# Four edits to a fp32 hybrid S5 / short-conv layer: the head's order, where six small loads are issued, how two tables lie in DRAM, and which engines do the last norms

## The chip, the cores and the metric

One NeuronCore of a Trainium2 chip runs the whole kernel. TensorE (PE) multiplies, VectorE (DVE), ScalarE (ACT) and GpSimd (POOL) work on vectors, and SyncE (SP), ACT and POOL issue DMAs. The metric is the device time of one execution in microseconds (us), as the median of several runs; less is better.

## The reference, cut to what matters

One layer of a latent generator: 512 latent rows `x` and 256 context rows `ctx` of 2048 channels, all fp32.

```
shift, scale, gate = split(silu(c) @ w_ada + b_ada)        # and the same for c_ctx
h  = layernorm(x)   * (1 + scale)   + shift                # (512, 2048)
hc = layernorm(ctx) * (1 + scale_c) + shift_c              # (256, 2048)
u, z_s5, v, bg, cg, z_cv = split(h @ w_in);  u_c = hc @ w_in[:, :1024]
# S5, 64 groups of 16 channels, 64 complex states, two directions
a_bar = exp(lam * dt);  b_bar = (a_bar - 1) / lam * b
states = scan(a_bar, b_bar, u), begun from the last context state
y_s5 = glu(Re(C states) + D u);  y_cv = bg * dwconv3(cg * v)
o = concat(y_s5 * silu(z_s5), y_cv * silu(z_cv)) @ w_out
out = layernorm(2**0.25 * x + gate * o) * ln_g + ln_b      # (512, 2048)
```

## The kernel before, in words

Every fp32 product is made of three matmuls on a high and a low part of either operand (`hi`/`lo` of the activations, `whi`/`wlo` of the weights). A weight tile arrives in `raw`, ScalarE copies it to `whi`, VectorE subtracts to get `wlo`. The weights of all projections form one list, `items`; SP loads them into five `raw` buffers in that order. Behind the head a planner with a cost model (`_Clock`) decides at build time where the vector work goes between the matmuls, so on the chip every engine runs a fixed list. All instructions pass through one helper line, so the profile gives nearly every one the same line, L137; tiles tell them apart.

**The head** (`head()`) is ordered by hand. Six row tiles are loaded into a ring of seven 1-MiB buffers (`wa`): four of `x`, two of `ctx`, and between and behind them the 32 pieces of the adaLN weights, two for each of the 16 channel blocks k. `stats(q)` are BN_STATS and the square root of row tile q, `norm(q)` the reciprocal steps and the scaling `wa<-wa`, `turn(q)` 16 PE transposes with their copies to `xl` or `xc`. `ada(k, hf)` multiplies a weight piece by silu(c) into `aps`; `combine(k)` copies that (`part`), transposes it and makes shift and scale (`ss`); `mod(k)` makes the high and low part of block k. `lat(k)` and `cxt(k, hf)` are the u projection of latent and context rows. A buffer of the ring is loaded again when its user has been issued (`fill`). `s5_params` (some hundred small VectorE instructions) is trickled into the loop over k by `some(us)`, ends in a table `PI`, whose transposes `WT` are stored to DRAM as `Wd`.

**Phase W** (`phase_w`) follows the head while PE works through the conv weights. For each of eight channel blocks i and of real and imaginary part r, `load_w` reads `pwt` from `Wd` and `load_b` reads `btt` from an input, 512 KB each and issued by POOL. In both, rows of 4 KB are repeated over partitions: the innermost contiguous run is 1024 floats, and the outer dimensions are [8 rows, 16 repeats] for `pwt` and [8 repeats, 16 rows] for `btt`. VectorE multiplies them into `wr`, `wi` (with `tm`), and PE makes the states. u passes through DRAM as `Ud`: ACT stores `ut`, POOL loads `uu`.

**The end.** `epi(q, b)` forms the residual of row tile q and column block b with its BN_STATS, `final(q)` normalizes the four blocks and stores them.

Of the kernel before, what the change touches and what calls it, by code (L numbers as in the profile page):

```python
# [8 lines left out]
F32 = mybir.dt.float32  # L9
# [3 lines left out]
OP = mybir.AluOpType  # L13
# [12 lines left out]
ALPHA = 2.0 ** 0.25  # L26
EPS = 1e-6
MAGIC = 12582912.0


class _Clock:
# [111 lines left out]
def tile_hybrid_s5_shortconv(  # L143
# [21 lines left out]
        return [dram.tile(shape, F32, name=f"{nm}{i}") for i in range(8)]  # L165

    Ud, Kd = spill("Ud", [L, P, NU]), spill("Kd", [2, P, 15 * H])
    Wd = dram.tile([L, 2, NG, P], F32, name="Wd")
    Gd, Zd, Od = spill("Gd", [P, 8, NCH]), spill("Zd", [P, SEQ]), spill("Od", [P, SEQ])

    hc_cm = pool(name="hc", bufs=1, side="right")
# [19 lines left out]
    def tt(out, a, b, op, e=None):  # L191
        (e or ve).tensor_tensor(out, a, b, op=op)
# [112 lines left out]
    def s5_params(hp, cps, lam, room):  # L305
# [146 lines left out]
        for j in range(4):  # L452
# [2 lines left out]
                pe.transpose(cps[:, n * P:(n + 1) * P], PI[:, 2 * j + n].rearrange("p r g -> p (r g)"), ident)  # L455
            ac.activation(WT[:, 2 * j:2 * j + 2], cps.rearrange("p (s c) -> p s c", s=2), AF.Copy)
            yield 0
        ac.dma_start(Wd.rearrange("s r g c -> (r g) s c"), WT)


    def head():
        with pool(name="head", bufs=1) as hp, \
                pool(name="hps", bufs=1, space=bass.MemoryType.PSUM) as ps:
            c2 = ss[:, :, 0]
            sp.dma_start(c2, c2_in)
            jp = ones.bitcast(I32)
            gp.iota(jp, pattern=[[1, P]], base=0, channel_multiplier=-1)
# [29 lines left out]
                load()  # L497
            lam = hp.tile([P, 3, NG], F32, name="lam")
            for t, src in ((bss, b_ss), (lam, lam_in), (cvw, cv_w), (cvb, cv_b), (bgl, b_glu), (dsk, dsk_in)):
                ac.dma_start(t, src)  # L500
            acc = [ps.tile([P, 512], F32, name=f"acc{i}") for i in range(7)]
            aps = ps.tile([P, 512], F32, name="aps")
            aps, cps = aps[:, 0:256], aps[:, 256:512]
# [7 lines left out]
            def stats(q):  # L511
                stt = hp.tile([P, 4, 6], F32, name="bst", tag="bst", bufs=2)
                mv = hp.tile([P, 2], F32, name="mv", tag="mv", bufs=3)
                for f in range(4):
                    ve.bn_stats(stt[:, f], rows["x", q][:, f * 512:(f + 1) * 512])
                    yield
                ve.bn_aggr(mv, stt)
                sts[q] = mv
                rss[q] = rstd_a(hp, mv[:, 1:2], epst)
                yield  # L520

            def norm(q):
                yield from rstd_b(rss[q], sts[q][:, 1:2])
                t = rows["x", q]
                ve.tensor_scalar(t, t, sts[q][:, 0:1], rss[q][:, 3:4], op0=OP.subtract, op1=OP.mult)

            def run(*gs):
                gs = list(gs)
                while gs:
                    for g in list(gs):  # L530
                        try:
                            next(g)
                        except StopIteration:
                            gs.remove(g)

            def turn(q):
                t = rows["x", q]
                for k4 in range(4):
                    b = acc[(4 * q + k4) % 7 if q < 4 else 3 + k4]
                    for k in range(4):  # L540
                        kk = k4 * 4 + k
                        pe.transpose(b[:, k * P:(k + 1) * P], t[:, kk * P:(kk + 1) * P], ident)
                    for k in range(4):
                        kk = k4 * 4 + k
                        dst = xl[kk][:, q * P:(q + 1) * P] if q < 4 else xc[kk][:, (q - 4) * P:(q - 3) * P]
                        if q == 5 and k % 2:
                            ve.tensor_copy(dst, b[:, k * P:(k + 1) * P])
                        else:
                            ac.activation(dst, b[:, k * P:(k + 1) * P], AF.Copy)
                used.add(("x", q))  # L550
                fill()

            def ada(k, hf):
                w = rows[k, hf].rearrange("p (k c) -> p k c", k=8)
                for j in range(8):
                    pe.matmul(aps[32 * (j % 4):32 * (j % 4) + 32], cs[:, hf * 8 + j], w[:, j],
                              start=hf == 0 and j < 4, stop=hf == 1 and j > 3)
                used.add((k, hf))
                fill()
# [43 lines left out]
            def mod_l(k):  # L603
                mod(k, [lpart])

            def mod_c(k):
                mod(k, [cpart])

            def split(n):
                while st["split"] < n:  # L610
                    j = st["split"]
                    hi, lo = pair()
                    r = raws.pop(j)
                    ac.activation(hi, r, AF.Copy)
                    tt(lo, r, hi.bitcast(F32), OP.subtract)
                    his[j] = (hi, lo)
                    st["split"] += 1

            run(stats(0))
            run(norm(0))  # L620
            run(stats(1))
# [3 lines left out]
            run(norm(2), stats(3))  # L625
            turn(2)
            ada(0, 0)
            run(norm(3))
            ada(0, 1)
            turn(3)  # L630
            comb = {k: combine(k) for k in range(KT)}
            next(comb[0])
            split(1)
            next(comb[0])
            mod_l(0)
            run(stats(4))
            ada(1, 0)
            ada(1, 1)
            next(comb[1])
            run(norm(4), stats(5))  # L640
            turn(4)
            lat(0, *his[0])
            next(comb[1])
            mod_l(1)
            split(2)
            run(norm(5))
            ada(2, 0)
            turn(5)
            lat(1, *his[1])
            ada(2, 1)  # L650
            next(comb[2])
            mod_c(0)
            split(3)
            next(comb[2])
            mod_l(2)
            mod_c(1)
            mod_c(2)
            lat(2, *his[2])
            cxt(0, 0, *his.pop(0))
            ada(3, 0)  # L660
            cxt(1, 0, *his.pop(1))
            ada(3, 1)
            next(comb[3])
            cxt(2, 0, *his.pop(2))
            ahead(3)
            next(comb[3])
            mod_l(3)
            mod_c(3)
            st["pos"] = 3
            params = s5_params(hp, cps, lam, lambda: (13, 0) in used)  # L670

            def some(us):
# [15 lines left out]
                cxt(k, hf, *w)  # L688
                st["pos"] += 1

            for k in range(4, KT):
                ada(k, 0)
                ada(k, 1)
                next(comb[k])
                half()
                if k == 4:
                    half()
                next(comb[k])
                half()
                mod(k, [lpart, cpart], lambda: some(1.3))  # L700
                some(1.3)
            while st["pos"] < 2 * KT:
                half()
                some(2.6)
# [35 lines left out]


    OB, uc = {}, {}
    head_order = [(k, hf) for hf in range(2) for k in range(3)] + [(k, hf) for k in range(3, KT) for hf in range(2)]
    for k, hf in head_order:
        add(w_u[k, :, hf * 512:(hf + 1) * 512], None)

# [201 lines left out]
    def phase_w():  # L948
# [5 lines left out]

        def load_w(i, r):
            pt[i, r] = s5.tile([P, 8, P], F32, name="pwt", tag="pwt", bufs=3)
            src = Wd[:, r, 8 * i:8 * i + 8]
            gp.dma_start(pt[i, r], bass.AP(tensor=src.tensor, offset=src.offset, ap=[[2 * NG * P, L], [0, H], [1, 8 * P]]))

        def load_b(i, r):  # L960
            bt[i, r] = s5.tile([P, 8, P], F32, name="btt", tag="btt", bufs=3)
            src = bt_in[i, :, r]
            gp.dma_start(bt[i, r], bass.AP(tensor=src.tensor, offset=src.offset, ap=[[0, L], [16 * P, H], [1, 8 * P]]))

        def states(i, wt):
            u = uu.pop(i)
# [359 lines left out]
    def final(q):  # L1326
        mv = cvp.tile([P, 2], F32, name="omv", tag="omv", bufs=2)
        ve.bn_aggr(mv, bst[:, q])
        sd = rstd_a(cvp, mv[:, 1:2], epst)
        yield 0  # L1330
        for _ in rstd_b(sd, mv[:, 1:2]):
            pass
        rs = sd[:, 3:4]
        nb = cvp.tile([P, 1], F32, name="onb", tag="onb", bufs=2)
        ve.scalar_tensor_tensor(nb, mv[:, 0:1], -1.0, rs, op0=OP.mult, op1=OP.mult)
        yield 0
        for b in (3, 0, 1, 2) if q > 2 else range(4):
            r = R[q, b]
            if q < 3 or b == 3:
                ac.activation(r, r, AF.Identity, scale=rs, bias=nb)  # L1340
                tt(r, r, lg[b], OP.mult, ve if q < 3 else gp)
                tt(r, r, lb[b], OP.add, gp)
            else:
                ve.scalar_tensor_tensor(r, r, mv[:, 0:1], lg[b], op0=OP.subtract, op1=OP.mult)
                ve.scalar_tensor_tensor(r, r, rs, lb[b], op0=OP.mult, op1=OP.add)
            sp.dma_start(out[q * P:(q + 1) * P, b * 512:(b + 1) * 512], r)
            yield 0

# [12 lines left out]
def _layout(inputs):  # L1361
# [32 lines left out]
    def bpar(re, im, perm):  # L1394
# [21 lines left out]
        "b_glu": asc(hg(g["b_glu"][0], 0).reshape(8, P).T),  # L1416
        "lam": asc(lam),
        "b": bpar(g["s5_b_re"], g["s5_b_im"], (1, 3, 0, 2, 4)),
        "bt": asc(np.stack([g["s5_b_re"][0], g["s5_b_im"][0]]).reshape(2, 2, 8, 8, 64, H)
                  .transpose(2, 5, 0, 3, 1, 4).reshape(8, H, 2, 8, P)),  # L1420
        "ct": asc(np.stack([c_ri, c_ri[::-1]]).transpose(1, 5, 2, 0, 3, 4).reshape(P, 2, 2, 8, 8, H)
                  .transpose(0, 3, 1, 2, 4, 5)),
        "dsk": dsk.reshape(P, 8, 2),
# [23 lines left out]
```

## Time and profile before

| | |
|---|---|
| median of 3 runs (1017.64 to 1020.67) | 1018.48 us |
| the profiled execution's own time | 1022.81 us |
| its span in the profile | 1021.0 us |
| mean granted TensorE clock | 0.969 |
| PE busy | 933.2 us (91%) |
| DVE busy | 674.8 us (66%) |
| ACT busy | 378.9 us (37%) |
| POOL busy | 146.6 us (14%) |
| HBM read, written | 177.37 MB, 16.12 MB |

The span is the profiled execution from its first to its last event; 1.8 us of its own time lie outside it. A share of 91% for PE says that the kernel as a whole is bound by TensorE; the other 88 us are a few waits, and where they lie decides what an edit elsewhere can give. The clock is the one granted by the throttle, 1.0 being 2.4 GHz and 0.5 being 1.2 GHz.

### The profile page before, as it was taken

The numbers are of one execution on the slowest core, as the hardware profiler recorded it, in microseconds if no ns is written. First come the engines' busy times: TensorE is split into PE (matmuls) and PEld (weight loads), VectorE is DVE, ScalarE is ACT, GpSimd is POOL, SyncE is SP. The second block draws the span as 40 slices with busy tenths as digits, with TensorE's granted clock in tenths as the row PEclk, the third lists the DMA queues.
The fourth block names the chain that finished last, engine by engine and source line by source line (L and its number), as shares of the span: only waits on it lengthen the run. The fifth ranks groups of instructions, "written<-read, shape, count | busy, mean of one in ns | idle before, by whom it ended". The sixth has DMA issues, their size and how long they took to land.

```text
span 1021.0 us, 15369 instructions
## 1 busy us (share of the span) xinstructions
PE 933.2 (91%) x5488; PEld 755.1 (74%) x5488; DVE 674.8 (66%) x1540; ACT 378.9 (37%) x671; POOL 146.6 (14%) x270
## 2 busy tenths in 40 slices
PE   2569799979999899999999999999999999999990
PEld 2447576857878788888888888888878877778780
DVE  5546995425877779989857556661245789782676
ACT  2523233313444332223345545465434432222321
POOL 0101040111112000000121202111200023300044
PEclk9879999989999999999999999999999999999996
DMA  8958774599899933333473735664686678854412
GB/s 322 364 186 332 284 299 148 147 231 225 201 220 183 214 98 113 105 109 114 126 201 100 212 85 165 153 165 127 181 276 215 226 260 306 309 158 152 145 67 99
DMA packets 104237, 194.53 MB, mean 191 GB/s; under 512 B 33376, under 2 KB 40672, under 8 KB 99296
## 3 DMA queue, kind: packets, MB, share of 16 engines
q1 hardware_dynamic: 69280, 110.14, 36.2%
q0 software_dynamic: 21328, 75.53, 24.8%
q10 hardware_dynamic: 13552, 7.88, 2.6%
q8 instruction: 43, 0.70, 0.3%
q14 instruction: 34, 0.28, 0.1%
HBM read 177.37 MB, written 16.12 MB: 190 GB/s over the span
## 4 chain that ended last, share of the span: by engine, by line
PE 68%; DVE 14%; DMA 10%; issue 4%; ACT 2%; SPq 0%; ACTq 0%; POOL 0%; DVEq 0%; POOLq 0%
PE mm L137 50%; PE bg L137 10%; PE acc L137 6%; DMA Ud<-ut 4%; DMA btt<-in_bt_dram 3%; DVE res L137 3%; PE aps L137 2%; DVE wlo L137 2%; DVE pt L137 2%; DVE tm L137 1%; DMA pwt<-Wd 1%; DVE bst L137 1%; DMA graw<-Gd 1%; DVE lo L137 1%; DMA wa<-in_x_dram 1%
## 5 line engine op out<-in xcount | busy, mean ns | idle before, releaser
L137 ACT ACTIVATE whi<-raw 128x512 fp32r<-128x512 f32 x276 | 171.5, 630 | 335.0 <-PE mm L137 225.6
L137 DVE TENSOR_TENSOR wlo<-raw,whi 128x512 fp32r<-128x512 f32 x276 | 188.2, 692 | 160.4 <-ACT whi L137 151.4
L137 PE MATMUL mm<-hi,wlo 128*128 128x512 f32 x720 | 283.6, 394 | 10.5 <-DVE wlo L137 10.3
L137 PE MATMUL mm<-hi,whi 128*128 128x512 f32 x720 | 285.9, 397 | 2.9 <-ACT whi L137 2.9
L137 PE MATMUL mm<-lo,whi 128*128 128x512 f32 x720 | 282.4, 392 | 0.0
L137 PEld LDWEIGHTS mm<-hi,wlo 128*128 128x128 f32 x720 | 136.4, 189 | 42.7 <-DVE wlo L137 13.9
L137 PEld LDWEIGHTS mm<-hi,whi 128*128 128x128 f32 x720 | 136.5, 190 | 35.0 <-ACT whi L137 3.9
L137 PEld LDWEIGHTS mm<-lo,whi 128*128 128x128 f32 x720 | 136.4, 189 | 27.5
L137 PE MATMUL acc<-hi,whi 128*128 128x256 f32 (+1 forms) x176 | 59.6, 338 | 2.9 <-ACT hi L137 2.9
L137 PE MATMUL acc<-lo,whi 128*128 128x256 f32 (+1 forms) x176 | 56.7, 322 | 0.5 <-DVE lo L137 0.5
L137 POOL DMA_DIRECT2D gw<-in_wada_g_dram x64 | 34.3, 537 | 154.5 <-DVE gacc L137 123.7
L137 PE MATMUL acc<-hi,wlo 128*128 128x256 f32 (+1 forms) x176 | 56.0, 318 | 0.0
L137 PE MATMUL acc<-ident,wa 128*128 128x128 f32 x96 | 18.8, 378 | 32.3 <-DVE wa L137 32.3
L137 DVE SCALAR_TENSOR_TENSOR gacc<-gw,cs,gacc 128x512 f32<-128x512 f32 x60 | 45.0, 750 | 1.2
L137 PE MATMUL aps<-wa,cs 128*32 128x256 f32 x512 | 35.1, 415 | 9.4 <-DVE ss L137 8.9
L137 PEld LDWEIGHTS acc<-hi,whi 128*128 128x128 f32 x176 | 34.5, 196 | 12.1 <-issue 5.0
L137 PEld LDWEIGHTS acc<-ident,wa 128*128 128x128 f32 x96 | 17.0, 202 | 34.4 <-DVE wa L137 28.1
L137 PEld LDWEIGHTS acc<-lo,whi 128*128 128x128 f32 x176 | 34.5, 196 | 3.2 <-DVE lo L137 1.0
L137 POOL TENSOR_TENSOR res<-res,lnp 128x512 f32<-128x512 f32 x14 | 23.3, 1683 | 94.3 <-DVE res L137 91.7
L137 PEld LDWEIGHTS acc<-hi,wlo 128*128 128x128 f32 x176 | 34.6, 197 | 2.3
L137 ACT ACTIVATE hxx<-vst 64x512 f32<-64x512 f32 x32 | 36.2, 1130 | 0.3
L137 PEld LDWEIGHTS aps<-wa,cs 128*32 128x32 f32 x512 | 15.6, 117 | 22.5 <-DVE ss L137 10.2
(211 smaller groups left out, 1549.0 us busy)
## 6 DMA issues: line engine op xcount, KB each, us to landing
raw<-in_w_m_dram SPq DMA_DIRECT2D x180, 256.0 KB, 2.9
wa<-in_wada_ss_dram POOLq DMA_DIRECT2D x29, 1024.0 KB, 7.7
gw<-in_wada_g_dram POOLq DMA_DIRECT2D x64, 256.0 KB, 5.5
raw<-in_w_out_dram SPq DMA_DIRECT2D x64, 256.0 KB, 3.6
raw<-in_w_u_dram SPq DMA_DIRECT2D x32, 256.0 KB, 6.3
btt<-in_bt_dram POOLq DMA_DIRECT2D x16, 512.0 KB, 16.0
pwt<-Wd POOLq DMA_DIRECT2D x16, 512.0 KB, 13.0
uu<-Ud POOLq DMA_DIRECT2D x16, 384.0 KB, 8.7
```

Source lines behind the costliest of these rows:

```text
L137: return f(*a, **k)
```

## The change

Four things are altered; the list of conv, glu and out projections and all vector work between them stay as they are, on every engine, instruction for instruction.

1. The head's order. The statistics of the first context tile now run between the steps of norm(3), those of the second before the first modulation, and turn(4) and turn(5) follow lat(0) with little between; the first context modulation is issued inside turn(5). The u projection goes by k and then by half (before: the first half of blocks 0 to 2, then their second half). The loop begins at k = 3, `some` is called with 1.0 us (before 1.3), and a raw weight is loaded at each `split`.
2. c2 is loaded into a contiguous piece of `ss` (before: pairs of floats 8 bytes long). Six small parameter loads are issued by POOL (before ACT).
3. `Wd` has four copies, written by four DMAs on ACT's queue, in rows with a pitch of 69,888 bytes (before 65,536). `pwt` reads outer dimensions [32 rows, 4 repeats]. `bt` is repeated eight times in the input, and `btt` is a plain load of 128 distinct rows.
4. The final norms use no POOL instruction: products and sums of rows are on DVE, and for the last tile (q = 3) one block goes by two DVE instructions, three by ACT and two DVE ones.

```
+NW = 4
+WP = 2 * NG * P + 1088
-    Wd = dram.tile([L, 2, NG, P], F32, name="Wd")
+    Wd = dram.tile([L, NW, WP], F32, name="Wd")
...
-        ac.dma_start(Wd.rearrange("s r g c -> (r g) s c"), WT)
+        for n in range(NW):
+            ac.dma_start(Wd[:, n, 0:2 * NG * P].rearrange("s (q c) -> q s c", c=P), WT)
...
-            c2 = ss[:, :, 0]
+            c2 = ss.rearrange("p k a m -> p (k a m)")[:, 0:2 * KT].rearrange("p (k m) -> p k m", m=2)
...
             for t, src in ((bss, b_ss), (lam, lam_in), (cvw, cv_w), (cvb, cv_b), (bgl, b_glu), (dsk, dsk_in)):
-                ac.dma_start(t, src)
+                gp.dma_start(t, src)
...
-                        if q == 5 and k % 2:
+                        if q == 5 and k4 > 1:
                             ve.tensor_copy(dst, b[:, k * P:(k + 1) * P])
...
+                    if q == 5 and k4 == 0:
+                        mod_c(0)
...
             ada(0, 0)
-            run(norm(3))
             ada(0, 1)
+            next(comb[0])
+            run(norm(3), stats(4))
+            split(1)
             turn(3)
-            comb = {k: combine(k) for k in range(KT)}
+            run(stats(5))
             next(comb[0])
-            split(1)
-            next(comb[0])
-            mod_l(0)
-            run(stats(4))
             ada(1, 0)
             ada(1, 1)
+            n4 = norm(4)
+            mod(0, [lpart], lambda: [next(n4) for _ in range(5)])
+            lat(0, *his[0])
+            run(n4)
             next(comb[1])
-            run(norm(4), stats(5))
+            split(2)
             turn(4)
-            lat(0, *his[0])
+            run(norm(5))
             next(comb[1])
-            mod_l(1)
-            split(2)
-            run(norm(5))
+            turn(5)
             ada(2, 0)
...
-            for k in range(4, KT):
-                ada(k, 0)
-                ada(k, 1)
+            for k in range(3, KT):
+                if k > 3:
+                    ada(k, 0)
+                    ada(k, 1)
+                    next(comb[k])
+                half()
                 next(comb[k])
                 half()
...
-                mod(k, [lpart, cpart], lambda: some(1.3))
-                some(1.3)
+                mod(k, [lpart, cpart], lambda: some(1.0))
+                some(1.0)
...
-            src = Wd[:, r, 8 * i:8 * i + 8]
-            gp.dma_start(pt[i, r], bass.AP(tensor=src.tensor, offset=src.offset, ap=[[2 * NG * P, L], [0, H], [1, 8 * P]]))
+            src = Wd[:, :, (8 * r + i) * 8 * P:]
+            gp.dma_start(pt[i, r], bass.AP(tensor=src.tensor, offset=src.offset,
+                                           ap=[[WP, L * NW], [0, H // NW], [1, 8 * P]]))
...
-            src = bt_in[i, :, r]
-            gp.dma_start(bt[i, r], bass.AP(tensor=src.tensor, offset=src.offset, ap=[[0, L], [16 * P, H], [1, 8 * P]]))
+            gp.dma_start(bt[i, r], bt_in[i, :, r])
...
-        for b in (3, 0, 1, 2) if q > 2 else range(4):
+        if q > 2:
+            for b in (0, 2, 3):
+                ac.activation(R[q, b], R[q, b], AF.Identity, scale=rs, bias=nb)
+        for b in (1, 0, 2, 3) if q > 2 else range(4):
             r = R[q, b]
-            if q < 3 or b == 3:
-                ac.activation(r, r, AF.Identity, scale=rs, bias=nb)
-                tt(r, r, lg[b], OP.mult, ve if q < 3 else gp)
-                tt(r, r, lb[b], OP.add, gp)
-            else:
+            e = ve
+            if q > 2 and b == 1:
                 ve.scalar_tensor_tensor(r, r, mv[:, 0:1], lg[b], op0=OP.subtract, op1=OP.mult)
                 ve.scalar_tensor_tensor(r, r, rs, lb[b], op0=OP.mult, op1=OP.add)
+            else:
+                if q < 3:
+                    ac.activation(r, r, AF.Identity, scale=rs, bias=nb)
+                    yield 0
+                tt(r, r, lg[b], OP.mult, e)
+                tt(r, r, lb[b], OP.add, e)
```

Three places show how instructions move. The first is DVE's list from the scaling of row tile 3 on; `wa` is a row tile, `bst` and `mv` are its statistics, `sd` its reciprocal steps. Before:

```order
L137 TENSOR_SCALAR wa<-wa,mv,sd 128x2048
L137 TENSOR_TENSOR wlo<-raw,whi 128x512
L137 TENSOR_REDUCE ss<-aps 128x4
L137 TENSOR_TENSOR ss<-ss,bss 128x4
L137 TENSOR_SCALAR ss<-ss 128x2
L137 TENSOR_SCALAR xl<-xl,ss 128x512
L137 TENSOR_TENSOR lo<-xl,hi 128x512
L137 BN_STATS bst<-wa 128x6 x4
```

And with the change, from the reciprocal of row tile 3 on:

```order
L139 RECIPROCAL sd<-sd 128x1
L139 BN_STATS bst<-wa 128x6
L139 TENSOR_SCALAR sd<-mv,sd 128x1
L139 BN_STATS bst<-wa 128x6
...
L139 BN_AGGR mv<-bst 128x2
L139 TENSOR_SCALAR wa<-wa,mv,sd 128x2048
L139 TENSOR_TENSOR wlo<-raw,whi 128x512
L139 BN_STATS bst<-wa 128x6 x4
L139 BN_AGGR mv<-bst 128x2
L139 TENSOR_REDUCE ss<-aps 128x4
```

The scaling of row tile 3 now stands behind the statistics of the first context tile, and the first `ss` behind those of the second; before, both stood ahead of them.

The second place is PE's list behind the first transposes of `part`; `acc` are the head's seven PSUM banks, and `hi,whi`, `lo,whi`, `hi,wlo` are the three matmuls of a product. Before:

```order
L137 MATMUL aps<-ident,part 128x128 x2
L137 MATMUL aps<-wa,cs 32x256 x16
L137 MATMUL acc_173<-ident,wa 128x128 x4
L137 MATMUL acc_174<-ident,wa 128x128 x4
L137 MATMUL acc_175<-ident,wa 128x128 x4
L137 MATMUL acc_176<-ident,wa 128x128 x4
L137 MATMUL acc_170<-hi,whi 128x512
```

And with the change:

```order
L139 MATMUL acc_172<-hi,wlo 128x512
L139 MATMUL acc_173<-ident,wa 128x128 x4
...
L139 MATMUL acc_176<-ident,wa 128x128 x4
L139 MATMUL aps<-ident,part 128x128 x2
L139 MATMUL acc_173<-ident,wa 128x128 x4
L139 MATMUL acc_174<-ident,wa 128x128 x4
L139 MATMUL acc_175<-ident,wa 128x128 x4
L139 MATMUL acc_176<-ident,wa 128x128 x4
L139 MATMUL aps<-wa,cs 32x256 x16
```

Before, the transposes of the first context tile stood ahead of the first latent products and those of the second behind them; now both stand behind these products, with one pair of `part` transposes between the two tiles.

The third place is ACT's list at the start; `cs` is silu(c), the first `sd` is the square root of the first statistics. Before:

```order
L137 ACTIVATE cs<-ss 128x16x2
L137 DMA bss<-in_b_ss_dram 128x32
L137 DMA lam<-in_lam_dram 128x192
L137 DMA cvw<-in_cv_w_dram 128x24
L137 DMA cvb<-in_cv_b_dram 128x8
L137 DMA bgl<-in_b_glu_dram 128x8
L137 DMA dsk<-in_dsk_dram 128x16
L137 ACT_TABLE_LOAD
L137 ACTIVATE sd<-mv,epst 128x1 x2
```

And with the change:

```order
L139 ACT_TABLE_LOAD
L139 ACTIVATE cs<-ss 128x16x2
L139 ACT_TABLE_LOAD
L139 ACTIVATE sd<-mv,epst 128x1 x2
L139 ACTIVATE xl<-acc_170 128x128 x4
```

Six DMA issues are gone from between the silu and the table that the square root needs.

## Rows read from the trace of the kernel before

**Rows 1.** The page, part 1: busy time and share of TensorE.

```profile
PE 933.2 (91%) x5488; PEld 755.1 (74%) x5488; DVE 674.8 (66%) x1540; ACT 378.9 (37%) x671; POOL 146.6 (14%) x270
```

**Rows 2.** Waits of PE: for whom, us in total, times, longest.

```profile
PE acc L137 <- DVE wa L137: 32.3, 5, 15.8
PE mm L137 <- DVE wlo L137: 10.3, 4, 5.9
PE aps L137 <- DVE ss L137: 8.9, 6, 3.2
```

**Rows 3.** Stretches: us, busy of each engine, granted clock, DMA share, GB/s.

```profile
50.00:75.00 25.00, 16.23 (x83) 11.90 (x82) 11.14 (x32) 7.61 (x22) 2.11 (x4) 0.77 0.53 190
...
100.00:125.00 25.00, 20.23 (x167) 15.81 (x165) 22.91 (x103) 6.48 (x12) 2.11 (x4) 0.93 0.84 317
...
200.00:225.00 25.00, 19.14 (x79) 15.42 (x78) 8.88 (x11) 3.76 (x6) 5.93 (x10) 0.89 0.98 229
225.00:250.00 25.00, 22.48 (x139) 17.84 (x138) 14.43 (x17) 8.58 (x17) 4.08 (x7) 0.91 1.06 230
...
300.00:350.00 50.00, 46.01 (x296) 37.39 (x296) 40.08 (x68) 18.39 (x36) 7.74 (x15) 0.97 0.97 201
350.00:975.00 625.00, 624.35 (x3315) 508.09 (x3314) 416.44 (x944) 244.47 (x364) 75.66 (x158) 1.00 0.56 170
```

**Rows 4.** Timeline of the first 16 us: start, duration, instruction, idle before.

```profile
11.37 0.34 ACTq L137 DMA_DIRECT2D dsk<-in_dsk_dram  x1
...
13.36 0.17 DVE L137 RECIPROCAL sd<-sd 128x1 f32<-128x1 f32 x1 [3.97 <-ACT sd L137]
...
14.39 1.35 DVE L137 TENSOR_SCALAR wa<-wa,mv,sd 128x2048 f32<-128x2048 f32 x1
```

**Rows 5.** Timeline of PE in the head.

```profile
15.79 3.67 PE L137 MATMUL acc<-ident,wa 128*128 128x128 f32 x16 [15.79 <-DVE wa L137]
...
31.57 1.97 PE L137 MATMUL acc<-ident,wa 128*128 128x128 f32 x16
...
46.66 3.68 PE L137 MATMUL acc<-ident,wa 128*128 128x128 f32 x16 [7.77 <-DVE wa L137]
...
59.43 3.42 PE L137 MATMUL acc<-ident,wa 128*128 128x128 f32 x16 [4.46 <-DVE wa L137]
...
83.61 1.93 PE L137 MATMUL aps<-wa,cs 128*32 128x256 f32 x32 [1.29 <-DVE ss L137]
```

**Rows 6.** The first load of context rows (issued at 19.5): KB, us to landing.

```profile
wa<-in_ctx_dram SPq DMA_DIRECT2D x1, 1024.0 KB, 10.7
```

**Rows 7.** The chain that ended last, where the head ends: start, us, what.

```profile
193.75 10.89 PE mm L137 x48
```

**Rows 8.** Two stretches, columns as in rows 3.

```profile
203.80:205.20 1.40, 1.40 (x8) 1.17 (x7) 0.00 (x0) 0.48 (x1) 1.40 (x4) 1.00 0.51 123
...
96.00:108.00 12.00, 12.00 (x119) 9.21 (x118) 11.01 (x44) 5.32 (x10) 2.11 (x4) 1.00 1.00 402
```

**Rows 9.** Timeline of DVE in phase W.

```profile
211.98 1.23 DVE L137 TENSOR_TENSOR wr<-pwt,btt 128x1024 f32<-128x1024 f32 x1 [3.46 <-DMA pwt<-Wd]
...
221.09 1.28 DVE L137 TENSOR_TENSOR wlo<-raw,whi 128x512 fp32r<-128x512 f32 x2
229.92 0.29 DVE L137 COPY ut<-uc 128x256 f32<-128x256 f32 x1 [7.55 <-DMA Ud<-ut]
```

**Rows 10.** DMA issues of the whole span: count, KB each, median us to landing.

```profile
btt<-in_bt_dram POOLq DMA_DIRECT2D x16, 512.0 KB, 16.0
...
Wd<-WT ACTq DMA_DIRECT2D x1, 512.0 KB, 3.2
```

**Rows 11.** The DMA of u issued at 205.35, in the same columns.

```profile
Ud<-ut ACTq DMA_DIRECT2D x1, 384.0 KB, 24.6
```

**Rows 12.** Instructions on `res`, the rows of the final norms: ns min/median/max.

```profile
L137 POOL TENSOR_TENSOR res<-res,lnp x14: 1281/1724/1772, 979.3 to 1009.5; 128x512 f32<-128x512 f32 x14
...
L137 DVE TENSOR_TENSOR res<-res,lnp x12: 691/874/1777, 978.5 to 1000.8; 128x512 f32<-128x512 f32 x12
```

More of the change, by code (lines that the diff above doesn't have):

```diff
@@ L617, in split @@
                     st["split"] += 1
+                    if st["load"] < st["split"] + 5:
+                        load()
+            comb = {k: combine(k) for k in range(KT)}
             run(stats(0))
@@ L627, in head @@
             ada(0, 0)
-            run(norm(3))
             ada(0, 1)
+            next(comb[0])
+            run(norm(3), stats(4))
+            split(1)
             turn(3)
-            comb = {k: combine(k) for k in range(KT)}
+            run(stats(5))
             next(comb[0])
-            split(1)
-            next(comb[0])
-            mod_l(0)
-            run(stats(4))
             ada(1, 0)
             ada(1, 1)
+            n4 = norm(4)
+            mod(0, [lpart], lambda: [next(n4) for _ in range(5)])
+            lat(0, *his[0])
+            run(n4)
             next(comb[1])
-            run(norm(4), stats(5))
+            split(2)
             turn(4)
-            lat(0, *his[0])
+            run(norm(5))
             next(comb[1])
-            mod_l(1)
-            split(2)
-            run(norm(5))
+            turn(5)
             ada(2, 0)
-            turn(5)
-            lat(1, *his[1])
             ada(2, 1)
+            cxt(0, 0, *his.pop(0))
             next(comb[2])
-            mod_c(0)
             split(3)
+            mod(1, [lpart, cpart])
             next(comb[2])
[L655 to L659, printed above, removed]
+            cxt(0, 1, *his.pop(1))
             ada(3, 0)
-            cxt(1, 0, *his.pop(1))
             ada(3, 1)
             next(comb[3])
[L664 to L669, printed above, removed]
+            mod(2, [lpart, cpart])
+            st["pos"] = 2
             params = s5_params(hp, cps, lam, lambda: (13, 0) in used)
@@ L689, in half @@
                 st["pos"] += 1
-            for k in range(4, KT):
-                ada(k, 0)
-                ada(k, 1)
+            for k in range(3, KT):
[4 more added lines that the diff above has]
+                half()
                 next(comb[k])
                 half()
[L696 to L699, printed above, removed]
-                mod(k, [lpart, cpart], lambda: some(1.3))
-                some(1.3)
+                mod(k, [lpart, cpart], lambda: some(1.0))
+                some(1.0)
             while st["pos"] < 2 * KT:
@@ L742, in tile_hybrid_s5_shortconv @@
     OB, uc = {}, {}
-    head_order = [(k, hf) for hf in range(2) for k in range(3)] + [(k, hf) for k in range(3, KT) for hf in range(2)]
+    head_order = [(k, hf) for k in range(KT) for hf in range(2)]
     for k, hf in head_order:
@@ L1418, in _layout @@
         "b": bpar(g["s5_b_re"], g["s5_b_im"], (1, 3, 0, 2, 4)),
-        "bt": asc(np.stack([g["s5_b_re"][0], g["s5_b_im"][0]]).reshape(2, 2, 8, 8, 64, H)
-                  .transpose(2, 5, 0, 3, 1, 4).reshape(8, H, 2, 8, P)),
+        "bt": asc(np.broadcast_to(np.stack([g["s5_b_re"][0], g["s5_b_im"][0]]).reshape(2, 2, 8, 8, 64, H)
+                                  .transpose(2, 5, 0, 3, 1, 4).reshape(8, 1, H, 2, 8, P), (8, L, H, 2, 8, P))
+                  .reshape(8, P, 2, 8, P)),
         "ct": asc(np.stack([c_ri, c_ri[::-1]]).transpose(1, 5, 2, 0, 3, 4).reshape(P, 2, 2, 8, 8, H)
```

## The prediction, as it was put on record

> **What bounds the kernel now.** I read the page first. TensorE is busy 91% of the span [rows 1], so time can only be won where it waits or runs at its lower clock; the 88 us that are left have to be found in places. The waits of PE, grouped by whom it waits for, name three causes: the scaled row tiles `wa` of the head's norms, 32.3 us in five waits; `wlo`, 10.3 us in four; the shift and scale `ss`, 8.9 us [rows 2]. The stretches then show where these lie. From 350 to 975 PE is busy 624.35 of 625 us at full clock, so nothing is to be had there. The head shows waits and clock loss together: from 50 to 75 PE is busy 16.23 of 25 us and the granted clock averages 0.77, that is, part of the stretch at the 0.5 level (1.2 GHz), and from 100 to 125 DVE itself is busy 22.91 of 25. A third stretch, 200 to 350, is phase W: the DMA share is 0.97 and more, but at only about 200 to 230 GB/s [rows 3], while in the middle of the head a share of 1.00 carries 402 GB/s [rows 8]. Whatever keeps the engines busy there, they move about half as much. Behind the last matmul lie some 25 us of norms and stores.
>
> The profiled execution took 1022.8 us for its span of 1021.0, 4.3 above the median of the runs. The sum is made against it.
>
> **The start: six issues leave ACT.** The reciprocal of row tile 0 waited 3.97 us for the square root, because ACT was still issuing the small loads, the last at 11.37, and then had to load a table [rows 4]. The statistics were there at 13.36 - 3.97 = 9.39. Without the issues the table is loaded in time and only the square root (0.3 us) remains: turn(0) goes from 15.79 [rows 5] to about 12.1. On POOL the six stand ahead of adaLN pieces whose buffers are not free before 30 us, so they cost nothing there. By itself this is worth 3.7 us at most, and little of it survives: the first context tile, issued at 19.5, lands 10.7 us later, at 30.2 [rows 6], behind loads that keep the queue full, and the new order makes row tile 3 wait for it.
>
> **The head's order.** In DVE's new list norm(3) is interleaved with the statistics of context tile 0. These can't begin before 30.2, take 4 x 0.7 us with the small steps between them, and the scaling of 1.35 [rows 4] follows: turn(3) moves from 31.57 [rows 5] to about 34.5, 3 us later. Then come the statistics of tile 1 (2.5 us) and `ss`, at 37.3; ada(1) 2 us; lat(0) 2 us; turn(4) at about 41.4 where it was 46.66; turn(5) at about 44.2 where it was 59.43 [rows 5]. The two waits before them, 7.77 and 4.46, shrink to well under 1, and with them goes the lower clock that follows long waits (16 transposes took 3.68 and 3.42 us there, 2 us at the full clock of 31.57).
>
> From turn(5) to ada(4) before took 83.61 - 59.43 = 24.2 us. Of it, 25 - 16.23 - 4.46 = 4.3 us is idle by [rows 3] plus 1.29 in front of ada(4) [rows 5], and a clock of 0.77 over 25 us is a loss of at most 5.8, of which I put 4.4 here: 14 us of work. The work left at ada(4) is almost the same (one `lat` more, one half `cxt` less). I add 4 us of waits of its own, since every block now needs its `ss`, its `hi` and `lo` in turn: ada(4) at 44.2 + 18 = 62, **21.6 us earlier**. Bounds: 26 with no wait at all; 12 if it keeps all of its present waits and clock loss and turn(4) waits again.
>
> From ada(4) to the first conv matmul before took 193.75 [rows 7] - 83.61 = 110.1 us. Here most of the 8.9 us for `ss` arise, behind the parameter instructions on a DVE that is nearly full. The change spreads these over 13 passes at 1.0 us in place of 12 at 1.3. I take 2 us back, less 0.6 for the work put off. Bounds: +8 with all waits and their clock gone; -6 if DMA becomes the limit (2.6 MB for each k at 402 GB/s are 6.5 us, at the 317 GB/s of 100 to 125 they are 8.3, where PE needs about 7). Head in all: **-23**, between -31 and -8.
>
> **The tables.** PE lost in phase W 5.86 + 2.52 + 3.99 us of idle and, by the clocks 0.89, 0.91 and 0.97, at most 2.75 + 2.25 + 1.5 us of speed [rows 3]: 18.9 us. The chain is plain on DVE: `wr` waits 3.46 for `pwt`, so the `wlo` queued behind it comes at 221.09, and PE waits 5.86 for that; `ut` then waits 7.55 for a store of u [rows 9] that took 24.6 us [rows 11], and ACT's next `whi` is late behind it. A `btt` needs 16.0 us to land [rows 10]. Does the new layout shorten this? Two rows speak. From 203.8 to 205.2 only 0.51 of the engines work, at 123 GB/s, although `wr` still waits for what they bring [rows 8]; both loads have an outer dimension of 8. And where the share is 0.97, each busy engine moves half of what it does in the head, where all rows read are distinct. Both are altered: outer dimensions of 32 and 128, four and eight times as many distinct rows. At the head's rate the 32 loads and the rest of the 31 MB of this stretch need some 80 us instead of 145, so the loads stand ready. I take **-16**, nearly all; what remains is the first pair, which still has to wait for the end of the head. Bounds: 0 (no faster) and -18.9.
>
> The Trainium skill (DMA: Bandwidth & Descriptors, Rules for kernel authors) says that an outermost dimension of fewer than 16, a broadcast too, confines a DMA to as many engines. By that rule the present loads run on half the engines and the sum holds; by the share of 0.97 alone the engines have no room, and the sum is that of the first rival. The 0.51 of [rows 8] agrees with the rule.
>
> The four stores of `Wd` cost ACT three more issues and DMA 1.5 MB, at 3.2 us each [rows 10], in a stretch with room (about 10 us of matmuls of the last two halves follow before PE needs new weights): nothing, 3 us if ACT is held.
>
> **The end.** POOL's part goes: an addition on POOL takes 1724 ns, on DVE 691, and beside POOL the DVE ones are drawn out to 1777 [rows 12]. For the last two tiles DVE does 8 instructions of 0.69 where it did 4 slow ones, so tile 3 begins no earlier, and its own six plus two end some 0.6 us sooner. **-0.6**, between +1.5 and -1.5.
>
> **Sum.** 23 + 16 + 0.6 = 39.6. From 1022.8 this gives 983.2, from the median 978.9. Where the 4.3 us between them lie isn't known; I say 981.
>
> **Rivals.**
> - *The loads stay slow.* If busy engines are what limits phase W, copies don't help, since as many bytes are moved. For it: the share of 0.97. Against: half the rate at that share, and 0.51 where loads are alone. It leaves some 2 of the 16 us: 995. That four repeats of one row still collide belongs here, the case in which the copies don't do what they are for.
> - *The head gives back.* DVE's list is served in order; with norm(3), both context statistics and `ss` behind two loads that land at 30 us and later, each late landing moves all that follows, and DMA or DVE may then limit each k. For it: DVE at 22.91 of 25, turn(3) 3 us later. Against: from 96 to 108 PE is busy 12.00 of 12.00 us under this very load [rows 8]. Head at -9: 995.
> - *Slower: the four stores hold up the first `pwt`.* All four must land before `load_w` may start, and DVE's `wr`, then `wlo`, then PE wait for it us by us. At 3.2 us each they land well before. If each took as long as the store of u did beside other loads, 24.6 us [rows 11], they would end 98 us after their issue, some 80 after `pwt` is due: 981 + 80 = 1061. It makes the kernel slower from 17 + 38 = 55 us on, 14 a store. Against: nothing else is heavy at that point.
>
> **How the numbers follow.** A difference under 0.3% can't be told from none here. Forecast 0.62; slow loads 0.14; head gives back 0.17; both (1009) 0.03; slow stores or some other loss of that size 0.04. The likeliest case reaches from 970 (31, 18.9 and 1.5 give 51, of which all at once is unlikely) to 992; the two next rivals lie at 995, so the range is 968 to 1000. Faster: 0.62 + 0.14 + 0.17 + 0.03 = 0.96, of which I take off 0.01 for mixed cases; same 0.02; slower 0.03.
>
> **What would show it.** turn(0) near 12 and turn(3) near 34.5; ada(4) near 62; first conv matmul near 170; no wait of PE for `wlo` between 200 and 350 at a DMA share well under 0.9; `btt` landing in under 10 us; last DVE instruction about 16 us behind the last matmul. It is wrong if turn(5) comes after 52, if PE waits for `ss` over 9 us in all, if the share in phase W stays near 1, or if a `pwt` wait stands in front of the first `wr`.

## The result, and the profile after

The changed kernel takes 972.86 us (median of 4 runs, 971.66 to 974.21), the kernel before 1019.58 us on the same chip (4 runs, 1017.64 to 1025.39). The ratio is 0.9533, with a 95% interval of 0.9491 to 0.9575. The forecast was 981, within 968 to 1000. The profiled execution of the changed kernel has a span of 972.4 us, 48.6 less than before (the medians differ by 46.7). Its three parts, read from the two traces:

| | before | after | difference | forecast |
|---|---|---|---|---|
| start to the first conv matmul | 193.6 | 164.8 | -28.8 | -23 |
| first conv matmul to the end of the last matmul | 802.8 | 788.4 | -14.4 | -16 |
| last matmul to the end of the span | 24.6 | 19.2 | -5.4 | -0.6 |

Waits of PE in the changed kernel, columns as in [rows 2]:

```profile
PE acc L139 <- DVE wa L139: 21.4, 5, 11.7
PE aps L139 <- DVE ss L139: 5.3, 3, 4.3
PE mm L139 <- ACT whi L139: 4.5, 2, 3.3
```

The wait for `wa` has lost 10.9 us, 4.1 of them in front of the first transposes; the 10.3 us for `wlo` have gone altogether. The wait for `whi` has grown, from 2.9 us in all to 4.5.

The stretches, columns as in [rows 3]:

```profile
50.00:75.00 25.00, 24.29 (x239) 18.78 (x238) 20.14 (x70) 10.53 (x19) 3.78 (x8) 1.00 1.02 415
75.00:100.00 25.00, 20.66 (x160) 15.96 (x159) 22.71 (x100) 6.70 (x13) 2.34 (x6) 0.86 0.64 247
...
175.00:200.00 25.00, 21.68 (x88) 17.00 (x87) 12.05 (x14) 5.40 (x9) 4.50 (x9) 0.93 0.88 308
200.00:225.00 25.00, 25.00 (x213) 20.90 (x212) 16.95 (x24) 12.03 (x25) 2.63 (x5) 1.00 0.75 241
225.00:250.00 25.00, 25.00 (x162) 20.63 (x161) 20.72 (x33) 9.56 (x18) 5.54 (x12) 1.00 0.78 249
...
300.00:350.00 50.00, 50.00 (x324) 41.60 (x323) 40.20 (x113) 18.85 (x36) 1.77 (x8) 1.00 0.39 120
```

From 50 to 75, where PE was busy 16.23 us at a clock of 0.77, it is busy 24.29 at full clock, and DMA runs at 415 GB/s. From 75 to 100 the parameter instructions fill DVE (22.71 of 25) and PE waits 4.3 us for `ss`, with the lower clock behind it. Phase W begins at 165 and stands still once, before 200; from 200 on PE never waits there, at a DMA share that is well below that of before.

The timeline of PE in the head, to be held against [rows 5]:

```profile
11.66 3.66 PE L139 MATMUL acc<-ident,wa 128*128 128x128 f32 x16 [11.66 <-DVE wa L139]
...
32.14 3.58 PE L139 MATMUL acc<-ident,wa 128*128 128x128 f32 x16 [5.09 <-DVE wa L139]
...
41.12 1.91 PE L139 MATMUL acc<-ident,wa 128*128 128x128 f32 x16
...
43.40 1.94 PE L139 MATMUL acc<-ident,wa 128*128 128x128 f32 x16 [0.15 <-DVE wa L139]
...
58.37 1.93 PE L139 MATMUL aps<-wa,cs 128*32 128x256 f32 x32
```

And the chain where the head ends, to be held against [rows 7]:

```profile
164.95 10.89 PE mm L139 x48
```

These are turn(0), turn(3), turn(4), turn(5) and ada(4): 4.1 us earlier, 0.6 later, 5.5, 16.0 and 25.2 earlier. From ada(4) on 106.4 us remain where there were 110.

The DMA issues of the whole span, columns as in [rows 10]:

```profile
btt<-in_bt_dram POOLq DMA_DIRECT2D x16, 512.0 KB, 6.4
pwt<-Wd POOLq DMA_DIRECT2D x16, 512.0 KB, 5.5
...
Ud<-ut ACTq DMA_DIRECT2D x8, 384.0 KB, 4.6
...
Wd<-WT ACTq DMA_DIRECT2D x4, 512.0 KB, 5.4
```

A `btt` lands in 6.4 us where it took 16.0. Before, `pwt` took 13.0:

```profile
pwt<-Wd POOLq DMA_DIRECT2D x16, 512.0 KB, 13.0
```

The time to landing begins at the issue, so it contains the time that a load spends among others.

The instructions on `res`, columns as in [rows 12]:

```profile
L139 DVE TENSOR_TENSOR res<-res,lnp x30: 674/691/694, 935.2 to 968.5; 128x512 f32<-128x512 f32 x30
```

No DVE product or sum is drawn out any more; the last one was 1777 ns at worst.

### The profile page after: what moved, and what is told of

It reads as the page before. It is cut to its first block, busy times and chain, and to the rows that moved or that the text cites. A ratio compares the mean times of both kernels' runs of the same rounds, so it can differ in the third digit from the quotient of the medians.

```text
span 972.4 us, 15375 instructions
## 1 busy us (share of the span) xinstructions
PE 919.2 (95%) x5488; PEld 748.1 (77%) x5488; DVE 673.7 (69%) x1554; ACT 379.8 (39%) x673; POOL 124.0 (13%) x262
## 4 chain that ended last, share of the span: by engine, by line
PE 85%; DVE 7%; DMA 5%; ACT 1%; issue 1%; ACTq 0%; SPq 0%; DVEq 0%
PE mm L139 62%; PE bg L139 12%; PE acc L139 8%; PE aps L139 3%; DVE res L139 3%; DMA Ud<-ut 2%; DMA wa<-in_ctx_dram 1%; DMA graw<-Gd 1%; DVE pt L139 1%; DMA wa<-in_x_dram 1%; DVE ept L139 1%; DVE sd L139 1%; ACTq L139 0%; DVE obst L139 0%; DVE wk L139 0%
## 5 line engine op out<-in xcount | busy, mean ns | idle before, releaser
L139 PE MATMUL aps<-wa,cs 128*32 128x256 f32 x512 | 32.7, 398 | 5.3 <-DVE ss L139 5.3
L139 PE MATMUL acc<-ident,wa 128*128 128x128 f32 x96 | 16.4, 344 | 21.4 <-DVE wa L139 21.4
L139 ACT ACTIVATE cvv<-mm 128x512 f32<-128x512 f32 x24 | 14.4, 598 | 47.1 <-PE mm L139 47.1
L139 PEld LDWEIGHTS acc<-ident,wa 128*128 128x128 f32 x96 | 14.9, 182 | 22.8 <-DVE wa L139 15.7
L139 DVE TENSOR_TENSOR sc<-MT,vst 128x128 f32<-128x128 f32 x128 | 31.3, 287 | 0.0
```

Source lines behind the costliest of these rows:

```text
L139: return f(*a, **k)
```

## The experiments

Each time is a median, beside the kernel before on the same chip (1018.8 to 1019.7 us in the four groups). The changed kernel itself was timed with the result alone and not again beside these runs; "more than the changed kernel" goes by its 972.86 us from there. The first four put one part of the change alone into the kernel before.

**The head's order alone**: of the change, the edits in `head()` from `turn` on, and `head_order`.

```
-            run(norm(3))
             ada(0, 1)
+            next(comb[0])
+            run(norm(3), stats(4))
+            split(1)
             turn(3)
+            run(stats(5))
...
-                mod(k, [lpart, cpart], lambda: some(1.3))
-                some(1.3)
+                mod(k, [lpart, cpart], lambda: some(1.0))
+                some(1.0)
...
-    head_order = [(k, hf) for hf in range(2) for k in range(3)] + [(k, hf) for k in range(3, KT) for hf in range(2)]
+    head_order = [(k, hf) for k in range(KT) for hf in range(2)]
```

> The kernel before with the new order of the head alone (six loads still on ACT, c2, tables and last norms as before). In the changed kernel the first conv matmul starts 28.8 us earlier than before. Theory: nearly all of it is the order, because row tile 3 and all behind it wait for the first context tile, whose landing is set by the queue of loads; then this run is 26 to 29 us faster, with the first conv matmul at 165 to 168. Rival: the earlier start carries through, since the first context tile also landed 2.4 us earlier with it; then this run gains only 22 to 25 us, with the first conv matmul near 170.

991.16 us, ratio 0.9705 (0.9667 to 0.9743), that is 28.5 us. The first conv matmul stands at 166.2, 27.4 earlier than before. The theory holds: the order alone does nearly all, and adding the start to it moves this point by only 1.4 us, to 164.8.

**The start alone.**

```
+            c2 = ss.rearrange("p k a m -> p (k a m)")[:, 0:2 * KT].rearrange("p (k m) -> p k m", m=2)
...
-                ac.dma_start(t, src)
+                gp.dma_start(t, src)
```

> The kernel before with the start alone: c2 into a contiguous piece, six small loads on POOL. Theory, as predicted: the first transposes come about 4 us earlier (near 12), but the stage behind them waits for loads, so little survives: 0 to 2 us faster, first conv matmul at 191 to 194. Rival: the old order passes the start on in full, 4 us faster, first conv matmul near 189.5.

1006.8 us, ratio 0.9869 (0.9831 to 0.9908): 12.9 us, three times what the larger of the two theories gave. The first conv matmul stands at 188.8, so 4.8 us are the start, passed on in full by the old order; the rival was right there. The other 8 lie where this edit changes no instruction. In its profiled execution, the fastest of its four (1004.0 us), the stretch from the first conv matmul to the last matmul is 793.2 us (before 802.8), with 6.9 us of PE waits for `wlo` and `whi` where before had 13.2; behind the last matmul it is 20.1 (before 24.6). The end has a cause that the trace shows: the closing DRAIN of POOL, of which the run of the last norms tells, lasted 2.6 us here in place of 10.8 and was over at 997.7, before the last store landed at 1001.0. Both are places that the rest of the change also empties, so the gains can't be added: the four single parts give some 61 us, the whole change 46.7. With the head's order and the last norms alone the same stretch was 799.7 and 800.7: with these slow loads it varies from kernel to kernel. What makes a certain kernel fall well or badly there was not found out, nor why its DRAIN is short.

**The tables alone**: `Wd` in four copies with padding, `btt` from 128 rows.

```
-    Wd = dram.tile([L, 2, NG, P], F32, name="Wd")
+    Wd = dram.tile([L, NW, WP], F32, name="Wd")
...
+                                           ap=[[WP, L * NW], [0, H // NW], [1, 8 * P]]))
...
+            gp.dma_start(bt[i, r], bt_in[i, :, r])
```

> The kernel before with the spread tables alone. From the first conv matmul to the last matmul the changed kernel needs 788.4 us, before needed 802.8. Theory: that is the tables' whole part and does not depend on the head, so this run is 13 to 16 us faster, PE waits under 4 us for wlo and whi between 200 and 350. Rival: part of the 14.4 comes from the head having ended earlier (raw weights further ahead, u stored earlier); then this run gains 8 us or less.

1004.1 us, ratio 0.9836 (0.9802 to 0.9869): 15.6 us. From the first conv matmul to the last matmul 787.2 us, against 788.4 in the changed kernel; PE waits 3.5 us for `whi` in all and not at all for `wlo`. The part stands by itself, as the theory said. Its profile gains 2.3 us more behind the last matmul, where the DRAIN lasted 8.5 us; this edit changes nothing there.

**The last norms alone**: the new loop in `final`.

```
-                tt(r, r, lg[b], OP.mult, ve if q < 3 else gp)
-                tt(r, r, lb[b], OP.add, gp)
...
+                tt(r, r, lg[b], OP.mult, e)
+                tt(r, r, lb[b], OP.add, e)
```

> The kernel before with the last norms on DVE and ACT alone. Theory A: what counted at the end is that POOL, after its last instruction, took 9 us to come to rest, until 4.9 us after the last store had landed; with POOL idle since long the span ends 1 us behind the last landing, and this run is 4.5 to 6 us faster. Theory B, the prediction's term: only the speed of the norms counts, 0.6 us faster (0 to 1.5).

1015.16 us, ratio 0.9941 (0.9911 to 0.9971; 12 runs, 1005.13 to 1020.05): 4.5 us. Behind the last matmul 19.5 us, where the kernel before has 24.6. That is theory A; the interval, 3.0 to 9.1 us, leaves out the 1.5 us that theory B allows at most. What stands behind it is an instruction that the trace has but no view lists: a DRAIN, with which POOL's program closes. In the trace of the kernel before it ends at 1020.24, 9.2 us behind POOL's last addition (1011.09), while the last store landed at 1015.40; in this run POOL came to rest at 899.5, long before the end.

**One POOL instruction put back at the end of the changed kernel.**

```
+        if q > 2:
+            last = cvp.tile([P, 1], F32, name="olast")
+            gp.tensor_copy(last, R[q, 3][:, 0:1])
```

> The changed kernel with one more POOL instruction, a copy of a single element per partition that reads the last finished block of the output and is used by nobody. Theory A: whatever POOL did last, it needs time to come to rest afterwards (2.6 to 10.8 us in the kernels so far), and the end of the program waits for it; the copy runs behind the last DVE instruction, so the span ends 1 to 9 us later than that of the changed kernel. Theory B: that time was due to the heavy additions on POOL; a tiny copy is done before the last store has landed, 0 us.

979.61 us (979.06 to 980.25), 6.7 more than the changed kernel. The timeline of POOL behind 960 has one line:

```profile
970.01 0.19 POOL L139 COPY olast<-res 128x1 f32<-128x1 f32 x1 [118.86 <-DVE res L139]
```

The copy is over at 970.2; the DRAIN behind it ends at 977.6, the last store has landed at 972.2, and the span ends at 978.4. A copy of one element per partition costs about as much as the additions did: theory A, as against heavy work on POOL. "Whatever POOL did last" is too wide, though. Behind the same additions the DRAIN lasted 10.8 us in the kernel before and in the run of the head alone, 8.5 with the tables alone and 2.6 with the start alone; here it is 7.6 (its record begins with the last instruction). So it does not follow from the last instruction alone, and what sets it was not tried.

**Distinct rows, but an outer dimension of 8.**

```
-            gp.dma_start(bt[i, r], bt_in[i, :, r])
+            src = bt_in[i, :, :, r]
+            gp.dma_start(bt[i, r], bass.AP(tensor=src.tensor, offset=src.offset, ap=[[(H + 1) * 16 * P, L], [16 * P, H], [1, 8 * P]]))
```

> The changed kernel, but the eight copies of each bt block lie with one spare row behind every 16, so that the load of btt has an outer dimension of 8 again while all of its 128 rows stay distinct. Theory A: an outer dimension of 8 keeps a load on 8 engines, and this counts: btt takes 9 us or more to land (6.4 in the changed kernel) and PE waits again for wlo in phase W, 3 to 8 us slower. Theory B: what made the loads slow was that one row was read by many packets at once; then btt lands in 6 to 8 us and the time is that of the changed kernel within 2 us.

980.29 us (975.26 to 983.83), 7.4 more. The DMA issues of this kernel:

```profile
btt<-in_bt_dram POOLq DMA_DIRECT2D x16, 512.0 KB, 12.6
pwt<-Wd POOLq DMA_DIRECT2D x16, 512.0 KB, 11.1
```

No row is read twice by `btt` here, as in the changed kernel; only the shape of the load is that of before. It takes 12.6 us in place of 6.4, and `pwt`, which is not touched, 11.1 in place of 5.5. PE waits for `wlo` again, at 192.9, which it doesn't in the changed kernel:

```profile
PE mm L139 <- DVE wlo L139: 4.8, 1, 4.8
```

That is theory A. A stretch of phase W in this kernel:

```profile
250.00:300.00 50.00, 50.00 (x425) 41.82 (x424) 41.17 (x60) 23.78 (x49) 9.09 (x19) 1.00 0.97 227
```

and the same stretch in the changed kernel:

```profile
250.00:300.00 50.00, 50.00 (x374) 41.86 (x374) 42.41 (x75) 21.97 (x44) 6.20 (x13) 1.00 0.64 210
```

Nearly the same GB/s, once at a share of 0.97 and once at 0.64. The share is made of the times of all packets, over 16 engines, and the packets take longer here: those of 4 KB on POOL's queue 267 ns in the mean in this stretch, in the changed kernel 185; those of 2 KB of the weights, whose loads are the same in both, 138 and 103. That the share can pass 1 (1.06 in [rows 3]) also says that it is no measure of engines at work. A share near 1 at a low rate does not show that all 16 are.

**`Wd` as before, `btt` new.**

```
-    Wd = dram.tile([L, NW, WP], F32, name="Wd")
+    Wd = dram.tile([L, 2, NG, P], F32, name="Wd")
...
+            gp.dma_start(pt[i, r], bass.AP(tensor=src.tensor, offset=src.offset, ap=[[2 * NG * P, L], [0, H], [1, 8 * P]]))
```

> The changed kernel with Wd as before (one copy, pitch 65,536 bytes, outer dimension 8, each row read 16 times); btt is the new plain load. Theory A and B both: half of the slow loads are back, pwt lands in 9 to 13 us, 4 to 10 us slower than the changed kernel. Rival C: with btt out of the way there is DMA enough, at most 2 us slower.

981.93 us (974.87 to 983.72), 9.1 more. Its `pwt`:

```profile
pwt<-Wd POOLq DMA_DIRECT2D x16, 512.0 KB, 11.6
```

One load of the two in the old shape slows both (`btt` 11.9), whichever it is. By the median rival C falls. But the profiled execution is the fastest of the four, 974.87 us, only 2.0 above the changed kernel's median, and in it, too, the loads are slow and the share is high:

```profile
250.00:300.00 50.00, 50.00 (x375) 41.69 (x374) 42.02 (x76) 21.77 (x43) 7.24 (x16) 1.00 0.94 229
```

PE waits for nothing in this stretch; from 160 to 350 it waits under 6 us in all (3.3 in the changed kernel). So loads of this shape cost 2 us in one execution and 8 to 11 in the other three; what decides it was not found out.

**Four copies without padding.**

```
-WP = 2 * NG * P + 1088
+WP = 2 * NG * P
```

> The changed kernel with four copies of Wd at the pitch of 65,536 bytes, that is, without the 4,352 bytes of padding. Theory: at this size the pitch doesn't matter, pwt lands in 5 to 6 us as in the changed kernel and the time is the same within 2 us. Rival: rows at a power of two collide, pwt takes 8 us or more and the time is 3 us or more longer.

974.50 us (972.96 to 975.52), 1.6 more with ranges that overlap, and `pwt` lands as fast as with padding:

```profile
pwt<-Wd POOLq DMA_DIRECT2D x16, 512.0 KB, 5.7
```

The padding does nothing that can be measured.

**Two copies.**

```
-NW = 4
+NW = 2
```

> The changed kernel with two copies of Wd in place of four: the load of pwt has an outer dimension of 16, and each row is read 8 times. Theory A (engines): with 16 all engines are in use, pwt lands as fast as with four copies, same time within 2 us. Theory B (one row read by many packets): pwt takes 8 us or more, 2 to 6 us slower.

978.44 us (976.91 to 980.99), 5.6 more than the changed kernel.

```profile
pwt<-Wd POOLq DMA_DIRECT2D x16, 512.0 KB, 7.3
```

Neither theory: faster than the 11.6 with an outer dimension of 8, but slower than with 32 and four repeats. From run to run the outer dimension and the repeats change together, so for `pwt` these times do not tell the repeated row from the shape; for `btt` the run with distinct rows did.

**Denser parameter portions.**

```
-                mod(k, [lpart, cpart], lambda: some(1.0))
-                some(1.0)
+                mod(k, [lpart, cpart], lambda: some(1.3))
+                some(1.3)
```

> The changed kernel with the parameter instructions handed out at 1.3 us a call, as before, in place of 1.0. Theory, the prediction's term: the denser portions hold up ss on DVE, PE waits 7 us or more for ss (5.3 in the changed kernel) and the time is 1 to 4 us longer. Rival: DVE has room in the new order, same time within 1 us.

977.96 us (975.38 to 979.27), 5.1 more. Waits of PE:

```profile
PE aps L139 <- DVE ss L139: 7.1, 5, 3.1
```

The first conv matmul comes at 169.4, 4.6 later than in the changed kernel. From 75 to 100 the granted clock is 0.80 too, where the changed kernel has 0.86. The theory holds, and the term is larger than it said.

**Row tile 3 ahead of the context statistics.**

```
-            run(norm(3), stats(4))
-            split(1)
+            run(norm(3))
             turn(3)
-            run(stats(5))
+            split(1)
+            run(stats(4))
+            run(stats(5))
```

> The changed kernel with norm(3) and turn(3) ahead of the statistics of the first context tile, not interleaved with them. DVE sat idle for 4.1 us before these statistics, waiting for the load. Theory: row tile 3 fits into that gap, turn(3) comes at 26 to 28 in place of 32.1 and without the 5.1 us wait, and DVE's run from the context load to turn(5) is 2 us shorter: 2 to 4 us faster. Rival: the context rows and adaLN pieces land when they land; turn(5) stays near 43 and the time is the same within 1 us.

975.31 us (972.93 to 977.23): no gain. The timeline of PE:

```profile
26.62 1.96 PE L139 MATMUL acc<-ident,wa 128*128 128x128 f32 x16
...
36.76 0.66 PE L139 MATMUL aps<-wa,cs 128*32 128x256 f32 x4 [7.95 <-DVE ss L139]
```

turn(3) comes at 26.6 as meant, and PE then waits 7.95 us in front of ada(1), since `ss` still stands behind both context statistics. The wait has moved, not gone; turn(5) comes at 44.2, not earlier. The rival holds.

**The same with `some(0.8)`.**

> As the run before, with the parameter instructions at 0.8 us a call. Theory: the wait of 4.3 us for ss near 91, where DVE is busy 22.7 of 25 us, shrinks to under 2, another 2 to 4 us faster. Rival: the instructions only end later, the same wait comes at a later block or PI is late, no gain or 1 to 3 us slower than the run before.

975.37 us (975.01 to 976.17). The wait for `ss` now comes one block later, at 99.9, and is 4.0 us long: the rival again. No version beat the changed kernel.

## Why the forecast was right in its direction, and where its size was off

The sum of the terms was 39.6 us and the two profiles differ by 48.6. Of the 9.0 us between them the head is 5.8, the end 4.8 and the tables -1.6: the head was undersized, the end left a mechanism out.

**The start.** turn(0) at 11.7 for 12.1; that little of the 3.7 us survives behind the new order is borne out by 1.4 us (166.2 to 164.8). "By itself 3.7 us at most" was too little: the old order passes 4.8 us on, since the loads behind it also begin earlier.

**The head's order.** The steps came as put: turn(4) 41.1 for 41.4, turn(5) 43.4 for 44.2. turn(3) came at 32.1 for 34.5 (34.6 in the run of the order alone), because the first context tile landed at 27.8, not at 30.2: the earlier start of the loads, which the text had left out. The term that was off is the waits between turn(5) and ada(4), taken too large: 4 us were added, and the trace has 0.7. So ada(4) stands at 58.4 for 62.

**The loop.** 1.4 us were taken back in all (2 for the spread of the parameters, less 0.6); measured are 3.6, and the run with 1.3 us a call puts the spread alone at 4.6. That DMA might become the limit of each k fell: from 50 to 75 it moves 415 GB/s, above the 402 on which the bound was made, and PE is busy 24.29 of 25 us.

**The tables.** -14.4 for -16, and 15.6 us in the run with the tables alone. The mechanism is the shape of the loads, as read from the stretch at a share of 0.51 [rows 8]: the run with distinct rows and an outer dimension of 8 gives back 7.4 us. The Trainium skill (DMA: Bandwidth & Descriptors, Rules for kernel authors) says that an outermost dimension of fewer than 16 confines a DMA to as many engines; that run agrees with the rule, though no view here counts the engines at work. The second reading of the text, many packets on one row, is not needed for `btt`; the two-copy run leaves some room for it at `pwt`. What remained of phase W's waits is not the first pair, as the text had it (the first `wr` waits 0.4 us for `pwt`), but one wait of 3.3 us for `whi`: ACT stood 9.45 us behind a store of u that took 17 us among the first loads. The Trainium skill (DMA: Bandwidth & Descriptors, Latency and other measured facts) tells of row pitches at large powers of two that slow a copy, from 207 GB/s at 512 KiB to 164 at 2 MiB and 103 at 4 MiB, and has no figure for 64 KiB; at this pitch the run without padding shows no such effect.

**The first rival** rested on the share of 0.97 as a sign that the engines were full. The two stretches at 0.97 and 0.64 with like rates show that this reading was the wrong one. **The second rival**, a head that gives back, came true in small: turn(3) is 0.6 us later than before, and PE waits 4.3 us for `ss` where DVE is busy 22.71 of 25; the head as a whole still won 28.8. **The third rival**, the stores of `Wd`: they landed in 3.3 to 7.2 us, and no `pwt` waited over 0.6 us for them.

**The end** is the step that failed: "-0.6, between +1.5 and -1.5" counted DVE instructions alone, and -5.4 came. The instructions were right (the last one ends 16.0 us behind the last matmul, 16.7 before). What was left out is POOL: before, its closing DRAIN outlasted the last store by 4.8 us. In the run of the start alone, where the same end had a short DRAIN, 20.1 us stand behind the last matmul, 0.9 more than in the changed kernel: there the term would have been nearly right. The gap could be seen before the change: the last store landed at 1015.4 and the span ended at 1021.0, and nothing in the views filled the 5.6 us.

## What to carry to other kernels

Follow the chain to the very end of the span: when the last store has landed and the program still runs, ask which engine worked last, and try letting GpSimd finish long before. Look at the outermost dimension of a load before its bytes, and don't take a DMA share near 1 for full engines when the GB/s are low. Where an engine serves its list in order, an instruction moved ahead of a wait only helps if what PE needs next moves ahead too.

## What the runs showed of the hardware that was not expected

GpSimd's closing DRAIN lasted 7.6 us behind a copy of one element per partition, and from 2.6 to 10.8 us, by the kernel, behind the same additions of 128x512. A load confined by its shape slowed the loads beside it as much as itself: `pwt` took 11.1 us in place of 5.5 when only `btt` had been reshaped. The kernel before varied from 1014.4 to 1027.1 us over all its 35 runs, the changed one from 971.7 to 974.2 over its four.
